# Two levels of HGRN2's token blocks in one product: 2 with 4, and 8 with 16

## The chip, the cores and the metric

The kernel runs on one core of one Trainium2 chip. The metric is the device time of one execution in microseconds; the median of three runs is taken.

## The reference, cut to what matters

One decoder layer: an RMSNorm, a product with `w_in`, two token mixers side by side (RWKV-7 with 16 heads of 64, HGRN2 with 8 heads of 128), a product with `w_out`, the residual and a last norm. There are 1024 tokens of 2048 numbers. The change touches HGRN2 alone:

```python
f = lb + (1.0 - lb) * sigmoid(f_raw)
k = 1.0 - f
Gc = cumsum(log(f))                      # inside chunks of 64 tokens
def step(S, inp):                        # one chunk
    qt, kt, vt, Gt = inp
    inter = einsum('bhtk,bhkv->bhtv', qt * exp(Gt), S)
    E = where(s <= t, exp(Gt[t] - Gt[s]), 0)
    A = einsum('bhtk,bhsk,bhtsk->bhts', qt, kt, E)
    intra = einsum('bhts,bhsv->bhtv', A, vt)
    kdec = kt * exp(G_last - Gt)
    S = S * exp(G_last) + einsum('bhsk,bhsv->bhkv', kdec, vt)
    return S, inter + intra
o = rmsnorm per head (inter + intra) * norm_g * silu(gate)
```

The decay between tokens s and t differs for each of the 128 key dimensions, so A is not one plain product of queries and keys.

## The kernel before, in words

Tokens go through in two halves of 512. The big products (`gemm`, L715) take a column block of 128 of `w_in` at a time, 16 steps each. A step is three matmuls of 128x512 (L732 to L734), since weights and activations are each split into a high and a low part (`whi`, `wlo`, `xs`); the split of the weights is done on ScalarE (L695, high) and VectorE (L705, low). After each step `step` (L788) calls every lane once: lanes are Python generators, one for the scan of RWKV, one for that of HGRN2, one for the group norm and so on. A lane writes down some instructions and then yields; `yield from range(H02)` lets H02 steps pass. So the order on each engine is set when the program is written out: by the lanes' yields and by the numbers in the table at L1041 to L1100. Each engine then runs its own row of instructions in that order and waits for the others by semaphores.

`hgrn_scan` (L246) does one head and one half, so it is called 16 times, eight per half. It works on 8 chunks of 64 tokens, four pairs (`c`) with two chunks (`x`) each. The score matrix A of each chunk is built by blocks. `k` and `qp` hold keys and queries with the decay inside their block of h tokens; `tot` holds the whole decay of each block. For each level the keys of the even blocks get the decay of the odd block behind them (L291, VectorE), the queries of the odd blocks that of the even one ahead (L294, GpSimd), the decays are multiplied in pairs (L298, VectorE), and the block is twice as large. At each level the queries of the odd blocks are multiplied with the keys (L306), and a masked copy (L315, `copy_predicated`, VectorE) takes the valid part from PSUM into AT. There are seven products in a scan: the first (L268) with 96 columns does the diagonal and the pairs of neighbours at once, five with 64 columns the levels 2, 4, 8, 16 and 32, and one (L306 again, four matmuls in place of eight) joins the two chunks of a pair. The 64 columns of each of the eight matmuls hold the odd blocks of both chunks of the pair, though only one of them belongs to the keys; masks leave out the rest.

AT is [128, 4, 128]; the two chunks of a pair lie on its diagonal, and the first product fills them with two masked copies each (L273, L277). Later L347 multiplies AT with the values, and L348 adds queries times state.

Beside it runs the RWKV scan (`rwkv_scan`, L429), eight chunks of 64 tokens one after the other (loop at L598). The prediction names its matmuls by letters: Q is L602 (and L603 beside it), which needs X; T is L611, which needs R, a copy of Q's result on ScalarE (L605); B is L617 (and L622), which needs X written from T by VectorE (L612) and ScalarE (L613); and the X of the next chunk is written from B by VectorE (L619), which also needs SW from GpSimd (L608). Between them stand steps of the big product: one from Q to T, two from T to B, one from B to the next Q. The products of HGRN2 fall between these. After the last chunk comes `rwkv_norm` (L631), and then the next head's LH (L458), which the four products of L467 need.

Of the kernel before, what the change touches and what calls it, by code (L numbers as in the profile page):

```python
# [39 lines left out]
CID, CPK, CBO, CRS, CIQ, NCST = 0, 128, 384, 512, 1024, 1280  # L40
LEVELS = (1, 2, 4, 8, 16, 32)


def shape_constants():
# [7 lines left out]
    c[:, CPK : CPK + 256] = np.concatenate([le, lt, lt, le], axis=1)  # L52
# [5 lines left out]
    m = np.zeros((P, P + 64 * len(LEVELS)), np.float32)  # L58
    m[:, :P] = np.eye(P)
    u = np.arange(64)  # L60
    for l, b in enumerate(LEVELS):
        lo = 2 * b * (u // b)
        m[:, P + 64 * l : P + 64 * (l + 1)] = (p[:, None] >= lo) & (p[:, None] < lo + b)
# [3 lines left out]
class Layer:  # L67
# [8 lines left out]
    def constants(self, cst, msk, vecs, ng):  # L76
# [3 lines left out]
        self.msk = cp.tile([P, P + 64 * len(LEVELS)], U8, name="msk")  # L80
# [42 lines left out]
    def scan_state(self, ctx):  # L123
# [4 lines left out]
        mf = sp.tile([P, P + 64 * len(LEVELS)], F32, name="mf", tag="BK")  # L128
# [7 lines left out]
        self.AT = sp.tile([P, 4, P], F32, name="AT")  # L136
        self.Ep = sp.tile([P, 8, 65], F32, name="Ep")
# [6 lines left out]
        for t in (self.AT, self.TT, self.LH, PX):  # L144
            nc.gpsimd.memset(t, 0.0)
# [100 lines left out]
    def hgrn_scan(self, i, half, f, k, q, v, g, y):  # L246
# [16 lines left out]
        AT = self.AT  # L263
        pl = self.pm()
        plv = pl[:, 0:384].rearrange("p (c n) -> p c n", c=nch)
        for c in range(nch):
            for x in (0, 1):
                nc.tensor.matmul(  # L268
                    plv[hp[x], c, :], lhsT=k[:, c * P + 64 * x : c * P + 64 * x + 64], rhs=q[:, c, x, :],
                    start=True, stop=True,  # L270
                )
        for x in (0, 1):
# [4 lines left out]
            nc.vector.copy_predicated(  # L277
                AT[hp[x], :, 64 * x + 1 : 64 * x + 64 : 2],
                self.msk[hp[x], P + 32 * x : P + 32 * x + 32].unsqueeze(1).broadcast_to([64, nch, 32]),
                plv[hp[x], :, 64:96],  # L280
            )
        yield from range(H01)
        tot = f
        for l in range(1, 8):
            b = 1 << l
            h = b // 2
            n = HT // b
# [13 lines left out]
            if b == P:  # L301
                break
# [743 lines left out]
H04 = 3  # L1046
H05 = 1
H06 = 3
H07 = 3
F00 = 1  # L1050
F01 = 1
F02 = 2
# [217 lines left out]
```

## Time and profile before

| | |
|---|---|
| median of 3 runs | 2367.86 us (2367.67 to 2368.54) |
| profiled execution, its time | 2369.59 us |
| profiled execution, its span | 2367.8 us |
| TensorE busy | 2323.3 us, 98% |
| VectorE busy | 1471.2 us, 62% |
| ScalarE busy | 951.3 us, 40% |
| GpSimd busy | 450.5 us, 19% |
| mean granted TensorE clock | 0.994 of full speed |

A busy TensorE is not a TensorE at its peak, since matmuls overlap and their ends are modelled; starts are the safer reading. The time of a wait is given with the engine that ended it.

### The profile page before, as it was taken

The page shows a single profiled execution, that of the slowest core. Times are in us where ns is not written, and L with a number is a line of the kernel's source. Part 1 is how long each engine was busy: PE and PEld are TensorE (multiplying, and loading weights), DVE is VectorE, ACT ScalarE, POOL GpSimd, SP SyncE. Part 2 cuts the span into 40 slices and gives each one's busy share as a digit, 9 for nine tenths or more (in the row PEclk, how much of TensorE's full clock was granted, in tenths as well). Part 3 has the DMA queues.
Part 4 walks back from the last instruction along what each step waited for, and adds up shares of the span by engine and source line. Part 5 has one row for each costly group of instructions (what it writes and reads, how often), then busy time and mean ns, then how long its engine had stood idle before and what let it go on. Part 6 is the DMA issues. An engine that isn't in the chain of part 4 may idle for free.

```text
span 2367.8 us, 35706 instructions
## 1 busy us (share of the span) xinstructions
PE 2323.3 (98%) x13067; PEld 1912.4 (81%) x13067; DVE 1471.2 (62%) x3104; ACT 951.3 (40%) x2188; POOL 450.5 (19%) x825
## 2 busy tenths in 40 slices
PE   8999999999999999999999999999999998999998
PEld 6888888888888888778888888888888887888888
DVE  5566666666666666656666766676766666435433
ACT  5334444434343434443434343434343434334323
POOL 3022222222121212220212121212121213101000
PEclk9999999999999999999999999999999999999999
DMA  6334334343434252624242424242424243434622
GB/s 185 85 92 92 104 86 109 83 117 82 110 99 128 78 140 62 167 67 105 69 105 68 105 69 104 70 104 70 98 75 96 78 118 116 178 117 142 249 98 98
DMA packets 379663, 249.59 MB, mean 105 GB/s; under 512 B 54368, under 2 KB 346336, under 8 KB 378336
## 3 DMA queue, kind: packets, MB, share of 16 engines
q1 hardware_dynamic: 378912, 243.12, 38.1%
q0 software_dynamic: 576, 4.19, 0.4%
q8 instruction: 103, 1.69, 0.3%
q14 instruction: 72, 0.59, 0.1%
HBM read 221.32 MB, written 25.95 MB: 104 GB/s over the span
## 4 chain that ended last, share of the span: by engine, by line
PE 85%; DVE 7%; ACT 4%; issue 2%; POOL 1%; DMA 1%; SPq 0%; DVEq 0%; POOLq 0%; ACTq 0%
PE g L732 18%; PE g L734 18%; PE g L733 17%; PE m L467 2%; PE m L306 2%; PE c L747 2%; PE c L746 2%; PE c L745 2%; DVE LH L458 2%; PE c L602 2%; PE m L747 1%; PE m L746 1%; PE m L745 1%; PE m L175 1%; PE c L611 1%
## 5 line engine op out<-in xcount | busy, mean ns | idle before, releaser
L732 PE MATMUL g<-xs,whi 128*128 128x512 f32 (+1 forms) x2160 | 904.1, 419 | 0.0
L734 PE MATMUL g<-xs,wlo 128*128 128x512 f32 (+1 forms) x2160 | 848.3, 393 | 1.2 <-DVE wlo L705 1.2
L733 PE MATMUL g<-xs,whi 128*128 128x512 f32 (+1 forms) x2160 | 844.9, 391 | 0.0
L705 DVE TENSOR_TENSOR wlo<-raw,whi 128x512 fp32r<-128x512 f32 (+1 forms) x646 | 469.8, 731 | 271.8 <-ACT whi L695 269.0
L695 ACT CAST whi<-raw 128x512 fp32r<-128x512 f32 (+1 forms) x648 | 393.2, 617 | 387.4 <-PE g L733 218.4
L734 PEld LDWEIGHTS g<-xs,wlo 128*128 128x128 f32 (+1 forms) x2160 | 404.3, 187 | 93.9 <-DVE wlo L705 2.9
L732 PEld LDWEIGHTS g<-xs,whi 128*128 128x128 f32 (+1 forms) x2160 | 406.0, 188 | 76.0 <-issue 0.3
L733 PEld LDWEIGHTS g<-xs,whi 128*128 128x128 f32 (+1 forms) x2160 | 406.6, 188 | 68.3
L608 POOL TENSOR_SCALAR SW<-Xs,Ep 64x64 f32<-64x64 f32 x256 | 135.6, 530 | 302.0 <-DVE Xs L619 290.5
L612 DVE TENSOR_SCALAR Xs<-c,D 64x64 f32<-64x64 f32 x128 | 35.3, 276 | 164.4 <-PE c L611 161.2
L549 DVE TENSOR_TENSOR Xw<-L,X 128x32 f32<-128x32 f32 (+15 forms) x256 | 114.5, 447 | 10.2 <-POOL L L544 5.3
L553 DVE TENSOR_REDUCE X<-Xw 128x16 f32<-128x32 f32 (+15 forms) x256 | 111.7, 436 | 8.8
L624 ACT COPY Y<-c 64x64 f32<-64x64 f32 x256 | 53.0, 207 | 154.6 <-PE c L622 152.4
L294 POOL TENSOR_TENSOR hqp<-hqp,tot 128x256 f32<-128x256 f32 x96 | 64.0, 666 | 193.7 <-PE m L306 163.8
L506 ACT COPY Xs<-m 64x256 f32<-64x256 f32 x64 | 23.6, 368 | 155.8 <-PE m L503 135.1
L619 DVE SCALAR_TENSOR_TENSOR Xs<-c,Ep,SW 64x64 f32<-64x64 f32 x240 | 67.3, 280 | 20.9 <-PE c L617 15.3
L537 POOL MEMSET L<- 128x16 f32 x32 | 3.1, 139 | 397.9 <-DMA L<-lsc 247.9
L567 POOL COPY PX<-Xr 32x256 f32<-32x256 f32 x32 | 12.7, 398 | 340.9 <-DVE Xr L565 340.3
L467 PE MATMUL m<-LH,BK 128*128 128x256 f32 x256 | 66.7, 383 | 7.5 <-DVE LH L458 7.5
L613 ACT ACTIVATE Xs<-c,D 64x64 f32<-64x64 f32 x128 | 39.6, 309 | 81.8 <-DVE Xs L612 79.7
L602 PEld LDWEIGHTS c<-Xs,LH 128*128 128x128 f32 x256 | 39.4, 188 | 39.1 <-DVE Xs L619 37.5
L705 POOL TENSOR_TENSOR xs<-xn,xs 128x512 fp32r<-128x512 f32 x24 | 34.0, 1421 | 190.7 <-ACT xs L944 188.6
(505 smaller groups left out, 3478.4 us busy)
## 6 DMA issues: line engine op xcount, KB each, us to landing
raw<-in_w_in SPq DMA_DIRECT2D x256, 512.0 KB
raw<-in_w_out SPq DMA_DIRECT2D x64, 512.0 KB
L<-lsc SPq DMA_DIRECT2D x16, 512.0 KB
xr<-in_x SPq DMA_DIRECT2D x32, 256.0 KB
xn<-y SPq DMA_DIRECT2D x32, 256.0 KB
out<-h SPq DMA_DIRECT2D x16, 512.0 KB
xr<-in_x SPq DMA_DIRECT2D x8, 512.0 KB
y<-yt SPq DMA_DIRECT2D x16, 256.0 KB
```

The source lines that it names most:

```text
L467: nc.tensor.matmul(pp[:, (c % 2) * 256 : (c % 2 + 1) * 256], lhsT=BK[:, c, :], rhs=LH[:, c].rearrange("p x n -> p (x n)"), start=True, sto ...
L549: nc.vector.tensor_tensor(w[:, :, :, 0:n], Lp[:, k, :, 2 * k :].unsqueeze(1).broadcast_to([P, 8, 2, n]), Xi[:, :, 2 * k :].unsqueeze(2).br ...
L553: nc.vector.tensor_reduce(Xi[:, :, 2 * k : 2 * k + 2].unsqueeze(3), w[:, :, :, 0:n], axis=AX.X, op=ALU.add)
L602: nc.tensor.matmul(ps[:, 0:P], lhsT=LH[:, c, 0, :], rhs=X[:, c, :], start=True, stop=True)
L608: nc.gpsimd.tensor_scalar_mul(SW[hp[h], :], X[hp[h], c, hp[h]], wc[hp[h]])
L695: nc.scalar.copy(hi[:, :, 0:n], raw)
L705: low()
L732: nc.tensor.matmul(ps[e], lhsT=hi[:, k, 0:n], rhs=x[:, 0, :], start=kk == 0, stop=False)
L733: nc.tensor.matmul(ps[e], lhsT=hi[:, k, 0:n], rhs=x[:, 1, :], start=False, stop=False)
L734: nc.tensor.matmul(ps[e], lhsT=lo[:, k, 0:n], rhs=x[:, 0, :], start=False, stop=kk == NK - 1)
L745: mm(ps, lhsT=x[:, 0, ts], rhs=hi, start=first, stop=False)
L746: mm(ps, lhsT=x[:, 0, ts], rhs=lo, start=False, stop=False)
```

## The change

The seven levels are no longer done one by one. The levels 2 and 4 share one product, and so do 8 and 16. For each pair, queries of three kinds are put side by side in `q`, 32 columns each for each chunk of 64 tokens: the odd blocks of the smaller level (kind 0), and, of the odd blocks of the larger level, the queries for the key block right ahead (kind 1) and for the one ahead of that (kind 2). Kinds 0 and 1 are copies on ScalarE, kind 2 is a multiply on GpSimd that adds the decay of the block between. The products are now taken for each chunk with its own queries alone, so level 32 has 32 columns. The masked copies write into a new tile AD, [128, 4, 64], in which the two chunks of a pair stand one below the other; two copies on ScalarE bring it into AT at the end. The constants tile and the masks become smaller, and the group norm uses two rows in place of three.

```diff
-LEVELS = (1, 2, 4, 8, 16, 32)
+LEVELS = ((2, 4), (8, 16), (32,))
...
-        for x in (0, 1):
+        def products(n, rhs):
+            pl = self.pm()
+            for c in range(nch):
+                for x in (0, 1):
+                    o = c * P + 64 * x
+                    nc.tensor.matmul(
+                        pl[hp[x], c * n : (c + 1) * n], lhsT=k[:, o : o + 64], rhs=rhs(c, x), start=True, stop=True
+                    )
+            return pl[:, 0 : nch * n].rearrange("p (c n) -> p c n", c=nch)
+
+        def take(pl, n, b, mask):
             nc.vector.copy_predicated(
-                AT[hp[x], :, hp[x]], self.msk[hp[x], hp[x]].unsqueeze(1).broadcast_to([64, nch, 64]),
-                plv[hp[x], :, 0:64],
+                AD.rearrange("p c (n e j) -> p c n e j", e=2, j=b)[:, :, :, 1, :],
+                self.msk[:, mask : mask + 32].rearrange("p (n j) -> p n j", j=b).unsqueeze(1).broadcast_to([P, nch, 32 // b, b]),
+                pl[:, :, n : n + 32].rearrange("p c (n j) -> p c n j", j=b),
             )
...
+        pl = products(96, lambda c, x: q[:, c, x, :])
+        nc.vector.copy_predicated(AD, self.msk[:, 0:64].unsqueeze(1).broadcast_to([P, nch, 64]), pl[:, :, 0:64])
+        take(pl, 64, 1, MONE)
         yield from range(H01)
...
+        for level in LEVELS:
+            b = level[0]
+            keys(b // 2)
+            queries(b // 2)
+            tot = totals(b)
+            yield from range(H02)
+            if len(level) == 1:
+                pl = products(32, lambda c, x: qp[:, c * P + 64 * x + 32 : c * P + 64 * x + 64])
+                yield from range(H03)
+                take(pl, 0, b, mask)
+                mask += 32
+                continue
+            nc.scalar.copy(kind(0, b), odd(b))
+            queries(b)
+            yield from range(H08)
+            nc.scalar.copy(kind(1, 2 * b), odd(2 * b))
+            n = 16 // b
+            nc.gpsimd.tensor_tensor(
+                kind(2, 2 * b), odd(2 * b),
+                tot.rearrange("p (g m e) -> p g m e", g=8, e=4)[:, :, :, 1:2].broadcast_to([P, 8, n, 2 * b]), op=ALU.mult,
             )
+            yield from range(H09)
+            pl = products(96, lambda c, x: q[:, c, x, :])
+            yield from range(H03)
+            take(pl, 0, b, mask)
+            take(pl, 32, 2 * b, mask + 32)
+            take(pl, 64, 2 * b, mask + 64)
+            mask += 96
+            keys(b)
+            tot = totals(2 * b)
+            yield from range(H03)
+        keys(32)
+        queries(32)
+        tot = totals(64)
+        yield from range(H02)
...
+        nc.scalar.copy(AT[0:64, :, 64:P], pl[0:64, 0:256].rearrange("p (c j) -> p c j", c=nch))
+        keys(64)
+        queries(64)
+        tot = totals(P)
+        for x in (0, 1):
+            nc.scalar.copy(AT[hp[x], :, hp[x]], AD[hp[x]])
+        yield from range(H02)
...
+H08 = 2
+H09 = 2
```

`keys`, `queries` and `totals` are the multiplies of L291, L294 and L298 under a name. The yields of a scan become a few more, so what stands behind them comes a little later among the steps of the big product.

On TensorE the prediction speaks of the fourth chunk of the RWKV scan. Before, from T to B:

```order
L611 MATMUL c<-R,TT 128x128
L306 MATMUL m<-hqp,hk 64x64 x8
L732 MATMUL g<-xs,whi 128x512
L733 MATMUL g<-xs,whi 128x512
L734 MATMUL g<-xs,wlo 128x512
L732 MATMUL g<-xs,whi 128x512
L733 MATMUL g<-xs,whi 128x512
L734 MATMUL g<-xs,wlo 128x512
L617 MATMUL c<-Xs,BKt 128x128
L622 MATMUL c<-Xs,PR 128x128
```

Now, from B to the next Q (L666 is B, L651 is Q):

```order
L666 MATMUL c<-Xs,BKt 128x128
L671 MATMUL c<-Xs,PR 128x128
L284 MATMUL m<-hqp,hk 64x32 x8
L781 MATMUL g<-xs,whi 128x512
L782 MATMUL g<-xs,whi 128x512
L783 MATMUL g<-xs,wlo 128x512
L651 MATMUL c<-Xs,LH 128x128
```

The product of level 32 has moved from between T and B to between B and the next Q; between T and B only two steps of the big product are left there.

On VectorE, the rows of the same chunk before, from its L612 to the update of X (L189 is the projection of k):

```order
L612 TENSOR_SCALAR Xs<-c,D_825 64x64
L315 COPY_PREDICATED AT<-msk,m 128x8x32
L705 TENSOR_TENSOR wlo<-raw,whi 128x512
L291 TENSOR_TENSOR hk<-hk,tot_1692 128x8x32
L298 TENSOR_TENSOR tot_1748<-tot_1692 128x8
L189 SCALAR_TENSOR_TENSOR k__1724<-g,omu,shift 128x512
L619 SCALAR_TENSOR_TENSOR Xs<-c,Ep,SW 64x64 x2
```

And now, from the update of X in the third chunk (L668 is L619, L661 is L612, L754 is wlo):

```order
L668 SCALAR_TENSOR_TENSOR Xs<-c,Ep,SW 64x64 x2
L291 COPY_PREDICATED AD<-msk,m 128x16x8
L291 COPY_PREDICATED AD<-msk,m 128x8x16 x2
L307 TENSOR_TENSOR hk<-hk,tot_1598 128x32x8
L315 TENSOR_TENSOR tot_1687<-tot_1598 128x32
L307 TENSOR_TENSOR hk<-hk,tot_1687 128x16x16
L315 TENSOR_TENSOR tot_1703<-tot_1687 128x16
L661 TENSOR_SCALAR Xs<-c,D_827 64x64
L754 TENSOR_TENSOR wlo<-raw,whi 128x512
L202 SCALAR_TENSOR_TENSOR k__1714<-g,omu,shift 128x512
L668 SCALAR_TENSOR_TENSOR Xs<-c,Ep,SW 64x64 x2
```

Three masked copies, two key multiplies and two totals now stand in one run ahead of L661, and none of them between L661 and the next L668.

On ScalarE, from the end of the chunks' preparation to the first chunk's R, before (L605 is R, L187 the shift, L202 the gate):

```order
L590 COPY TT<-m 32x8x32 x2
L695 CAST whi<-raw 128x512
L187 ACTIVATE shift<-g,vec 128x512
L202 ACTIVATE th<-g__1524 128x512
L605 COPY R<-c 128x128
```

And now, up to the second chunk's R (L335 and L338 collect kinds 0 and 1):

```order
L639 COPY TT<-m 32x8x32 x2
L744 CAST whi<-raw 128x512
L335 COPY hq<-hqp 128x8x32
L200 ACTIVATE shift<-g,vec 128x512
L338 COPY hq<-hqp 128x8x32
L215 ACTIVATE th<-g__1524 128x512
L654 COPY R<-c 128x128
L744 CAST whi<-raw 128x512
L662 ACTIVATE Xs<-c,D_827 64x64
L673 COPY Y<-c 64x64 x2
L654 COPY R<-c 128x128
```

Two collecting copies stand ahead of the first chunk's R; the second chunk's R has none ahead of it.

On GpSimd, at the end of the scan before (L336 clears the first state, L184 is the first column of the shift for r, L356 and L357 HGRN2's norm, L638 the first of the group norm):

```order
L356 TENSOR_SCALAR hss<-hss 128x4
L357 TENSOR_TENSOR hss<-hss,mhalf 128x4
L184 MEMSET shift 128x1
L193 COPY carry<-shift 128x1
L638 TENSOR_SCALAR gn<-gn 128x8
```

And now:

```order
L197 MEMSET shift 128x1
L206 COPY carry<-shift 128x1
L405 TENSOR_SCALAR hss<-hss 128x4
L406 TENSOR_TENSOR hss<-hss,mhalf 128x4
L687 TENSOR_SCALAR gn<-gn 128x8
```

The shift's memset has moved ahead of HGRN2's norm.

## Rows read from the trace of the kernel before

**Rows 1.** The page: busy time, share of the span and instructions of TensorE.

```profile
PE 2323.3 (98%) x13067; PEld 1912.4 (81%) x13067; DVE 1471.2 (62%) x3104; ACT 951.3 (40%) x2188; POOL 450.5 (19%) x825
```

**Rows 2.** TensorE's timeline: start, length (us), line; the idle time before it in brackets.

```profile
156.84 0.42 PE L602 MATMUL c<-Xs,LH 128*128 128x128 f32 x2
...
158.01 0.38 PE L611 MATMUL c<-R,TT 128*128 128x128 f32 x2
...
171.36 0.49 PE L602 MATMUL c<-Xs,LH 128*128 128x128 f32 x2 [0.16 <-DVE Xs L619]
...
209.72 1.10 PE L467 MATMUL m<-LH,BK 128*128 128x256 f32 x4 [0.71 <-DVE LH L458]
```

**Rows 3.** The list of waits, whole span: us in total, times, longest.

```profile
PE m L467 <- DVE LH L458: 7.5, 14, 0.7
...
PE c L602 <- DVE Xs L619: 6.3, 15, 1.9
```

**Rows 4.** TensorE's timeline around one group of eight 64-column products.

```profile
148.63 0.40 PE L734 MATMUL g<-xs,wlo 128*128 128x512 f32 x1
148.96 0.69 PE L306 MATMUL m<-hqp,hk 128*64 128x64 f32 x16
149.57 0.50 PE L732 MATMUL g<-xs,whi 128*128 128x512 f32 x1
149.91 0.40 PE L733 MATMUL g<-xs,whi 128*128 128x512 f32 x1
150.14 0.40 PE L734 MATMUL g<-xs,wlo 128*128 128x512 f32 x1
```

**Rows 5.** TensorE's timeline: 32-column products of RWKV, then the 96-column group.

```profile
142.91 1.11 PE L578 MATMUL m<-Xc,PX 64*64 64x32 f32 x16
143.96 0.88 PE L268 MATMUL m<-hq,hk 128*64 128x96 f32 x16
144.77 0.50 PE L732 MATMUL g<-xs,whi 128*128 128x512 f32 x1
```

**Rows 6.** TensorE's timeline: the scan's last group, four products.

```profile
172.92 0.68 PE L306 MATMUL m<-hqp,hk 128*64 128x64 f32 x8
```

**Rows 7.** Groups by line and shape, whole span: busy us, mean ns, idle before.

```profile
L315 DVE COPY_PREDICATED AT<-msk,m 128x256 f32<-128x256 uint8 x80 | 40.2, 502 | 39.6 <-PE m L306 39.6
...
L277 DVE COPY_PREDICATED AT<-msk,m 64x128 f32<-64x128 uint8 x32 | 14.1, 440 | 1.1
...
L298 DVE TENSOR_TENSOR tot<-tot 128x128 f32<-128x128 f32 x16 | 4.7, 296 | 0.0
...
L261 ACT COPY hq<-hqp 128x256 f32<-128x256 f32 x16 | 6.9, 428 | 2.7 <-DVE hqp L260 2.7
...
L294 POOL TENSOR_TENSOR hqp<-hqp,tot 128x256 f32<-128x256 f32 x96 | 64.0, 666 | 193.7 <-PE m L306 163.8 <-issue 29.9
```

**Rows 8.** VectorE's timeline, the second chunk of the first scan.

```profile
158.50 0.28 DVE L612 TENSOR_SCALAR Xs<-c,D 64x64 f32<-64x64 f32 x1 [1.79 <-PE c L611]
159.05 0.44 DVE L315 COPY_PREDICATED AT<-msk,m 128x256 f32<-128x256 uint8 x1 [0.28 <-PE m L306]
159.39 0.97 DVE L705 TENSOR_TENSOR wlo<-raw,whi 128x512 fp32r<-128x512 f32 x1
160.29 0.41 DVE L291 TENSOR_TENSOR hk<-hk,tot 128x256 f32<-128x256 f32 x1
160.62 0.18 DVE L298 TENSOR_TENSOR tot<-tot 128x32 f32<-128x32 f32 x1
160.84 0.60 DVE L619 SCALAR_TENSOR_TENSOR Xs<-c,Ep,SW 64x64 f32<-64x64 f32 x2
```

**Rows 9.** ScalarE's timeline, R of the same chunk.

```profile
157.34 0.27 ACT L605 COPY R<-c 128x128 f32<-128x128 f32 x1 [0.58 <-PE c L602]
```

**Rows 10.** VectorE's timeline at the end of the first scan.

```profile
194.45 0.75 DVE L189 SCALAR_TENSOR_TENSOR r__1955<-g,omu,shift 128x512 f32<-128x512 f32 x1 [2.83 <-POOL shift L184]
```

**Rows 11.** GpSimd's timeline at the same place.

```profile
193.32 1.05 POOL L357 TENSOR_TENSOR hss<-hss,mhalf 128x4 f32<-128x4 f32 x1
```

More of the change, by code (lines that the diff above doesn't have):

```diff
@@ L38 @@
 )
-CID, CPK, CBO, CRS, CIQ, NCST = 0, 128, 384, 512, 1024, 1280
-LEVELS = (1, 2, 4, 8, 16, 32)
+CID, CPK, CBO, CRS, CIQ, NCST = 0, 128, 256, 384, 896, 1152
+LEVELS = ((2, 4), (8, 16), (32,))
+MONE, MLEV, NMSK = 64, 96, 320
 def shape_constants():
@@ L57, in shape_constants @@
     c[:, CIQ : CIQ + 256] = iq.reshape(P, 256)
[L58 to L63, printed above, removed]
+    m = np.zeros((P, NMSK), np.float32)
+    k = (p % 64)[:, None]
+    m[:, 0:64] = k == np.arange(64)
+    u = np.arange(32)
+    between = lambda lo, n: (k >= lo) & (k < lo + n)
+    m[:, MONE : MONE + 32] = between(2 * u, 1)
+    o = MLEV
+    for b in LEVELS:
+        m[:, o : o + 32] = between(2 * b[0] * (u // b[0]), b[0])
+        o += 32
+        if len(b) == 2:
+            lo = 2 * b[1] * (u // b[1])
+            m[:, o : o + 32] = between(lo + b[0], b[0])
+            m[:, o + 32 : o + 64] = between(lo, b[0])
+            o += 64
     return c, m
@@ L136, in scan_state @@
         self.AT = sp.tile([P, 4, P], F32, name="AT")
+        self.AD = sp.tile([P, 4, 64], F32, name="AD")
         self.Ep = sp.tile([P, 8, 65], F32, name="Ep")
@@ L143, in scan_state @@
         self.Pb, self.Xh = PX[0:64], PX[64:P]
-        for t in (self.AT, self.TT, self.LH, PX):
+        for t in (self.AT, self.AD, self.TT, self.LH, PX):
             nc.gpsimd.memset(t, 0.0)
@@ L262, in hgrn_scan @@
         yield from range(H00)
[L263 to L266, printed above, removed]
-            for x in (0, 1):
[L268 to L272, printed above, removed]
+        AT, AD = self.AT, self.AD
+        def products(n, rhs):
[7 more added lines that the diff above has]
+            return pl[:, 0 : nch * n].rearrange("p (c n) -> p c n", c=nch)
@@ new lines, in hgrn_scan, with keys, queries @@
+        pairs = lambda x: x.rearrange("p (n e) -> p n e", e=2)
+        blocks = lambda x, j: x.rearrange("p (n e j) -> p n e j", e=2, j=j)
+        def keys(h):
+            kv, n = blocks(k, h)[:, :, 0, :], HT // (2 * h)
+            nc.vector.tensor_tensor(kv, kv, pairs(tot)[:, :, 1:2].broadcast_to([P, n, h]), op=ALU.mult)
+        def queries(h):
+            qv, n = blocks(qp, h)[:, :, 1, :], HT // (2 * h)
+            nc.gpsimd.tensor_tensor(qv, qv, pairs(tot)[:, :, 0:1].broadcast_to([P, n, h]), op=ALU.mult)
@@ new lines, in hgrn_scan @@
+        keys(32)
+        queries(32)
+        tot = totals(64)
+        yield from range(H02)
+        pl = self.pm()
+        for c in range(nch):
+            nc.tensor.matmul(
+                pl[0:64, c * 64 : (c + 1) * 64], lhsT=k[:, c * P : c * P + 64], rhs=qp[:, c * P + 64 : (c + 1) * P],
+                start=True, stop=True,
+            )
+        yield from range(H03)
+        nc.scalar.copy(AT[0:64, :, 64:P], pl[0:64, 0:256].rearrange("p (c j) -> p c j", c=nch))
+        keys(64)
```

62 lines of the change are left out of this document (14 added, 48 removed).

## The prediction, made before the changed kernel had run

> **What bounds the kernel now.** I read the page first. TensorE is busy for 98% of the span, the next engine, VectorE, for 62% [rows 1]. That share flatters TensorE, because a matmul of the big products is drawn 0.39 us long while the next one starts 0.23 us later [rows 4]. So I went on to the timeline of TensorE alone, and read start times, not lengths. Nearly everywhere one matmul starts as soon as the one before lets it. Where TensorE waits, the waits are few and come back with each head: at the start of a chunk of the RWKV scan for the state X from VectorE, and at L467 for LH from VectorE [rows 2]. The list of waits puts them at 6.3 us in 15 times and 7.5 us in 14 times [rows 3]; each is 0.16 us longer in truth, because the matmul before it is drawn that much too long (0.39 less 0.23). TensorE's instruction stream is the bound, and work taken out of it comes off the span unless a wait takes its place. The gain is therefore worked out in two parts: TensorE work removed, and waits that go or come.
>
> **The products of the HGRN2 scan.** A product group of eight 64-column matmuls costs more than its own time, because the switch to half-width products breaks the rhythm of the big ones. From the L734 before it to the second big matmul behind it 1.28 us pass [rows 4]; without the group these would be two steps of 0.23, 0.46 us. So a group costs 0.82 us. The 96-column group L268 occupies 0.81 us from its first start to the next big matmul [rows 5], the 64-column one 0.61 [rows 4]: 0.20 more, so 1.02 us. The last group has four products, all on one half of the array, and is drawn 0.68 us long [rows 6], the group of eight on both halves 0.69 [rows 4]: also 0.82. The changed kernel's eight 32-column products are not in this trace. Taking 0.20 per 32 columns off again gives 0.62; no saving gives 0.82. L578 has 32 columns and needs 1.05 us for its 16 passes [rows 5], not less than the 64-column group, so I take 0.82 and keep the other 3.2 us (16 x 0.20) for the range.
> Before, one scan has one group of 96 columns and six at 0.82: 1.02 + 4.92 = 5.94 us. After, three of 96 columns, one of 32 and the last: 3.06 + 0.82 + 0.82 = 4.70. That is 1.24 us less, and with 16 scans **19.8 us** of TensorE work, all of it in line with the big products.
>
> **What the other engines get.** ScalarE gains per scan four copies that collect queries, like L261 at 0.43 us, and two copies from AD to AT of half the partitions, which I price at the same 0.43. GpSimd gains two multiplies like L294 at 0.67 [rows 7]. VectorE keeps nine masked copies, seven of them now of 128 elements a partition. Such a copy lies between 0.30 (a 128-element multiply, L298) and 0.44 us (the 128-element masked copy L277) [rows 7]; the present 256-element one takes 0.50 on average. None of these engines is full, so only places count where TensorE waits for them.
> The Trainium skill, "VectorE: DVE Perf Modes", section on the TRN2 errata, gives 120 cycles plus one per element at 0.96 GHz for a copy out of PSUM, so 0.26 us as an estimate for 128 elements; the 0.44 us of L277 contradicts it here. By the page the three copies in a row would be 0.5 us shorter than by that row and could delay nobody, which would make the sum 0.6 us larger; the sum below uses neither value, but steps between the rows.
>
> *Three masked copies in a row.* They follow each of the two combined products, on VectorE, where the RWKV chain's updates of X queue behind them. Steps from start to start there: masked copy 0.34, wlo 0.90, key multiply 0.33, total 0.22 [rows 8]; a short masked copy then takes 0.20 (0.34 less the 0.14 between 0.44 and 0.30) to 0.34. First place, the chunk with the first group: T (L611) at 0; VectorE is free at 0.77 (L612 starts 0.49 behind T and takes 0.28) [rows 2, 8]; wlo to 1.67, masks to 2.27 or 2.69, key and total to 2.82 or 3.24. The product B (L617) now stands at 0.22 + 1.02 + 6 x 0.23 = 2.62, and X can be updated 0.49 later, at 3.11. So VectorE is in time or 0.13 late. Its two updates take 0.60, to 3.71 or 3.84, and Q (L602) is due at 2.62 + 0.45 + 0.69 = 3.76. A wait of 0 to 0.08, so 0 to 1.3 us in all; I take 0.6. Second place: masks, two keys and two totals stand between the update of X in the third chunk and L612 of the fourth, 1.7 to 2.1 us, where VectorE now idles for 1.79 [rows 8]. L612 may be 0.3 late, but it ends 0.77 behind T where nothing is late, and B comes 0.22 + 6 x 0.23 = 1.60 behind T even in a chunk without a group. Nothing.
>
> *ScalarE in front of R.* R (L605) must be copied between Q and T. It ends at 157.34 + 0.27 = 157.61 and T starts at 158.01 [rows 2, 9]: 0.40 to spare. In the first chunk two of the collecting copies stand ahead of R, with the shift of the gate between them, and the second waits for GpSimd. TensorE also comes there 0.82 earlier, as one group ahead of it is gone. Bounds: nothing, or both copies, 0.86 us. In favour of the low end, VectorE's gate projection, behind which R waits, loses a masked copy, a key multiply and a total ahead of it, 0.34 + 0.33 + 0.22 = 0.89. I take 0.2 a scan, **3.2 us** lost; the range keeps 13.8. The other two collecting copies come behind L613 and behind R, where nobody waits for ScalarE. Products wait for GpSimd's last multiply, but it has two steps of the big product, 1.4 us, for 0.67.
>
> *Waits that go.* Twelve of the 15 waits for X are like that at 171.36 [rows 2]: VectorE has the masked copy, wlo, key, total and the projection of k ahead of X. In the new order wlo and the projection alone stand there, and a 32-column group (0.82) stands on TensorE ahead of Q. 12 x (0.16 + 0.16) = **3.8 us** go. The wait at L467 is the end of a long chain: VectorE's projection of r waits 2.83 us for a memset on GpSimd [rows 10], which stands behind the power of hss, 1.05 us [rows 11], which waits for HGRN2's outputs. All of the group norm and then LH come behind. In the new order this memset stands ahead of hss, so the norm starts up to 2.8 us earlier; HGRN2's end is later by two or three steps and gives about 1 us back. The wait is 0.71 + 0.16 = 0.87, so I let it go: 7.5 + 14 x 0.16 = **9.7 us**.
>
> **The sum.** 19.8 + 3.8 + 9.7 - 0.6 - 3.2 = 29.5 us. The profiled execution took 2369.6, the median of the runs is 2367.9; the difference is a sum against one execution of the same program, so I carry it over to the median: 2367.9 - 29.5 = 2338.4, **2338 us**.
>
> **Rivals.**
> *Only the work goes.* The waits for X and LH are ends of latency chains, and a faster TensorE reaches them sooner, or other late ends stand just behind. Then 19.8 - 0.6 - 3.2 = 16.0 remain: 2352 us. Against it speaks that the new order takes known causes away, not only slack.
> *VectorE's bunches become the bound.* The three masks take 0.44 each without overlap, 0.3 us more in each of two places, 9.6 us, and the old waits stay: 16.0 - 9.6 = 6.4 us, 2361. L277's 0.44 speaks for it, the 1.79 us of idle time against. The Trainium skill, "TensorEngine Tiling (Array Packing)", section Performance Considerations, warns of this: tiling speeds up the products and not the copies out of PSUM. The trace shows masked copies within the engine's idle time so far.
> *The chain becomes the bound, no change.* The second and fourth chunks lose their group, and if the chain Q, R, T, X, B, X took as long as TensorE did with it, 1.24 us a scan would come back as waits: about 2368. Against it: R is ready 0.77 behind Q [rows 2, 9], VectorE's half of X 0.77 behind T and its update 1.09 behind B [rows 8], 2.6 us in all, while a chunk without a group still has four steps of three big matmuls on TensorE, 12 x 0.23 = 2.8 us, and its own five small pairs beside them.
> *Slower: ScalarE is stopped by GpSimd.* A collecting copy stands ahead of R and waits in ScalarE's queue for a multiply of 0.67 us, with R, the whi casts and the Y copies behind it. One such place costs 0.43 + 0.67 - 0.40 = 0.70 us. From two of the four places a scan (1.4 against 1.24) the kernel is slower; at all four it loses 16 x 2.8 = 44.8 and ends at 2367.9 - 19.8 + 44.8 = 2393. The order shows both copies of the second pair away from R, which speaks against it.
>
> **How the numbers follow.** Forecast 0.64, only work 0.22, bunches 0.06, no change 0.04, slower 0.04. The forecast's own low end: 29.5 + 3.2 (32 columns) + 3.8 (no new wait) + about 5 for smaller waits of the same kind that I did not list, 41.5: 2326. The upper end of the range must take in the second case and the higher price of R in it, so 2358. What lies above (bunches, no change, slower) and a little of the other two make the 2 in 10. A measurement of this kernel can tell about 0.2% from no change, 4.7 us: faster 0.92, same 0.04, slower 0.04.
>
> **What would show it.** On TensorE's timeline three groups of 0.81 us a scan in place of one, and two of 0.61 in place of six; if the 32-column one is shorter, the price was too high. In the list of waits LH at L467 near zero, X below 5 us, R up by at most a few us. A product waiting for GpSimd or ScalarE, T waiting for R by more than 0.5 us in each scan, or VectorE's updates of X starting more than 0.3 us behind B would show the terms wrong. If LH still waits 7 us, the chain behind HGRN2's end was read wrongly, and the second case holds.

## The result, and the profile after

The changed kernel takes **2330.4 us** (median of five runs, 2329.9 to 2330.6) against 2368.5 us for the kernel before on the same chip; the ratio is 0.9837 with a 95% interval of 0.9824 to 0.9851. The prediction was 2338 us, so it named about three quarters of the gain: 29.5 us of 38. The profiled span fell from 2367.8 to 2328.8 us.

The page's line of busy times answers to [rows 1]. TensorE has 512 matmuls less and is as "busy" as before; VectorE's busy time fell by 18 us, ScalarE's and GpSimd's rose:

```profile
PE 2293.4 (98%) x12555; PEld 1897.1 (81%) x12555; DVE 1452.8 (62%) x3104; ACT 981.4 (42%) x2284; POOL 471.0 (20%) x858
```

The list of waits of TensorE answers to [rows 3] (us in total, times, longest). LH is not in it any more, and X (L651, which was L602) has 3 waits in place of 15. New in the list is T (L660) at its head, put down partly to SW from GpSimd and partly to R from ScalarE:

```profile
PE c L660 <- POOL SW L657: 3.5, 7, 0.5
PE c L660 <- ACT R L654: 2.5, 6, 0.5
PE c L651 <- DVE Xs L668: 1.5, 3, 0.6
```

The product groups on TensorE's timeline (start, length, line), the answer to [rows 4] and [rows 5]. The combined 96-column group goes from 152.73 to the next big matmul at 153.54, 0.81 us; the 32-column group from 168.67 to 169.25, 0.58, hardly less than the 0.61 of 64 columns:

```profile
152.34 0.46 PE L660 MATMUL c<-R,TT 128*128 128x128 f32 x2 [0.41 <-ACT R L654]
152.73 0.88 PE L284 MATMUL m<-hq,hk 128*64 128x96 f32 x16
153.54 0.50 PE L781 MATMUL g<-xs,whi 128*128 128x512 f32 x1
...
168.67 0.66 PE L284 MATMUL m<-hqp,hk 128*64 128x32 f32 x16
169.25 0.50 PE L781 MATMUL g<-xs,whi 128*128 128x512 f32 x1
...
206.67 1.03 PE L516 MATMUL m<-LH,BK 128*128 128x256 f32 x4
```

The last of these rows is the four products that waited 0.71 us for LH in [rows 2]: no idle time stands before it now. The groups of instructions by line and shape show the new masked copy, and ScalarE's collecting copies, at the prices the prediction bounded with [rows 7] (0.30 to 0.44, and 0.43):

```profile
L291 DVE COPY_PREDICATED AD<-msk,m 128x128 f32<-128x128 uint8 x128 | 42.7, 334 | 3.9 <-PE m L284 0.2
...
L335 ACT COPY hq<-hqp 128x256 f32<-128x256 f32 x32 | 13.2, 412 | 0.4
L338 ACT COPY hq<-hqp 128x256 f32<-128x256 f32 x32 | 13.1, 408 | 6.5 <-POOL hqp L311 3.2 <-POOL shift L197 3.2
```

**Where the 39 us went.** The list of waits counts only what exceeds the drawn ends, so I also went over all of TensorE's starts. For every stretch of other matmuls between two big ones I took the time from the start of the big matmul ahead to the start of the second one behind, less two steps of 0.2265 us. The fastest stretch of a kind (over several kernels) is its work, and what another of the kind takes more, if over 0.04 us, is a wait, put down to the place at which the stretch begins. In us over the whole run:

| | before | after | difference |
|---|---|---|---|
| work of the other matmuls | 469.3 | 451.5 | -17.8 |
| waits at Q, most of them for X | 21.9 | 6.7 | -15.2 |
| wait for LH | 10.8 | 0 | -10.8 |
| wait of the group norm's first product for Y | 1.7 | 0 | -1.7 |
| waits at T | 5.2 | 9.2 | +4.0 |
| waits at B | 0 | 3.2 | +3.2 |
| all other waits | 19.5 | 20.0 | +0.5 |
| all of it, with what is under 0.04 us | 531.5 | 492.6 | -38.9 |

The total agrees with the spans (-39.0). So a little under half is work, and the rest is waits: 28 us gone, 7 us new. The experiments ask where these waits come from, and what the work consists of.

### The profile page after: what moved, and what is told of

Its sections match the earlier page's. It is cut to its first block, busy times and chain, and to the rows that moved or that the text cites. A ratio compares the mean times of both kernels' runs of the same rounds, so it can differ in the third digit from the quotient of the medians.

```text
span 2328.8 us, 34832 instructions
## 1 busy us (share of the span) xinstructions
PE 2293.4 (98%) x12555; PEld 1897.1 (81%) x12555; DVE 1452.8 (62%) x3104; ACT 981.4 (42%) x2284; POOL 471.0 (20%) x858
## 4 chain that ended last, share of the span: by engine, by line
PE 89%; DVE 4%; DMA 3%; issue 2%; ACT 1%; POOL 1%; SPq 0%; POOLq 0%; DVEq 0%; ACTq 0%
PE g L781 19%; PE g L783 19%; PE g L782 19%; PE m L516 2%; PE m L284 2%; PE c L796 2%; PE c L794 2%; PE c L795 2%; PE m L796 1%; PE m L794 1%; PE m L795 1%; PE c L660 1%; PE c L651 1%; PE g L794 1%; PE g L796 1%
## 5 line engine op out<-in xcount | busy, mean ns | idle before, releaser
L754 DVE TENSOR_TENSOR wlo<-raw,whi 128x512 fp32r<-128x512 f32 (+1 forms) x646 | 449.1, 698 | 296.9 <-ACT whi L744 295.6
L602 DVE TENSOR_REDUCE X<-Xw 128x16 f32<-128x32 f32 (+15 forms) x256 | 111.8, 437 | 8.8
L661 DVE TENSOR_SCALAR Xs<-c,D 64x64 f32<-64x64 f32 x128 | 35.2, 275 | 123.7 <-PE c L660 93.6
L668 DVE SCALAR_TENSOR_TENSOR Xs<-c,Ep,SW 64x64 f32<-64x64 f32 x240 | 67.5, 281 | 57.2 <-PE c L666 51.9
L754 POOL TENSOR_TENSOR xs<-xn,xs 128x512 fp32r<-128x512 f32 x24 | 34.1, 1423 | 188.7 <-ACT xs L993 186.5
L654 ACT COPY R<-c 128x128 f32<-128x128 f32 x128 | 33.8, 264 | 80.4 <-PE c L651 80.4
```

The source lines that it names most:

```text
L602: nc.vector.tensor_reduce(Xi[:, :, 2 * k : 2 * k + 2].unsqueeze(3), w[:, :, :, 0:n], axis=AX.X, op=ALU.add)
L754: low()
```

## Experiments

**1. The LH chain in the kernel before.** The prediction said that a memset of one column on GpSimd, behind the power of hss [rows 11], holds VectorE [rows 10] and with it LH. Here only that column moves to VectorE:

```diff
-        if half == 0:
-            nc.gpsimd.memset(s[:rows, 0:1], 0.0)
-        else:
-            nc.gpsimd.tensor_copy(s[:rows, 0:1], self.carry[:rows, col : col + 1])
         nc.scalar.activation(s[:rows, 1:], ps[:rows, :], AF.Copy, scale=mu[:rows])
         yield
+        if half == 0:
+            nc.vector.memset(s[:rows, 0:1], 0.0)
+        else:
+            nc.vector.tensor_copy(s[:rows, 0:1], self.carry[:rows, col : col + 1])
         nc.vector.scalar_tensor_tensor(
```

> The kernel before, in which one instruction of the token shift changes its engine and place: the first column (a memset in the first half, a copy of the carry in the second) is written by VectorE right ahead of the multiply-add that reads it, and no longer by GpSimd. The products of HGRN2 stay as they were. Theory: the wait of L467 for LH (9.7 us with the modelled overlap) is the end of a chain that hangs on this memset alone, which stands in GpSimd's queue behind the power of hss; so it goes without any change of the products, and some of the small waits at T and at the gate with it: 9 to 12 us less than before, about 2358. Rival: the group norm's own start at HGRN2's outputs sets LH; then the wait stays near 9 us and the time near 2368.

Measured: 2366.0 us, ratio 0.9987 (0.9978 to 0.9997). The wait for LH is gone from the list of waits, as the theory says, but the time is only 3.4 us shorter, not 10. Its list has what came in exchange:

```profile
PE c L602 <- DVE Xs L619: 10.7, 16, 1.9
...
PE c L611 <- ACT R L605: 5.1, 13, 0.7
```

By the accounting above LH fell from 10.8 to 1.6 us and the norm's wait from 1.7 to 0, while T rose from 5.2 to 8.7 and X by 5.8. VectorE's timeline in the first chunk shows why: masked copy, wlo, key and total run without a gap up to the column, so the gate's projection, behind which R waits, is later by it:

```profile
151.50 0.28 DVE L298 TENSOR_TENSOR tot<-tot 128x128 f32<-128x128 f32 x1
151.72 0.06 DVE L186 MEMSET shift<- 128x1 f32 x1
151.91 0.75 DVE L189 SCALAR_TENSOR_TENSOR g__1524<-g,omu,shift 128x512 f32<-128x512 f32 x1
```

From the total to the projection 0.41 us pass, where the kernel before needs 0.21 (151.35 to 151.56). The cause of the LH wait is shown; that it can be removed at no price is not.

**2. The same edit in the changed kernel.** In the changed kernel T waits, and the timelines of the engines in the first chunk offer two causes. The first: on GpSimd the column of the gate's shift (L197) stands behind the query multiply, which waited for ScalarE's collecting copy.

```profile
149.61 0.94 POOL L311 TENSOR_TENSOR hqp<-hqp,tot 128x256 f32<-128x256 f32 x1 [6.42 <-ACT hq L335]
150.49 0.10 POOL L197 MEMSET shift<- 128x1 f32 x1
...
150.62 0.75 DVE L202 SCALAR_TENSOR_TENSOR g__1524<-g,omu,shift 128x512 f32<-128x512 f32 x1 [0.68 <-POOL shift L197]
...
150.58 0.41 ACT L338 COPY hq<-hqp 128x256 f32<-128x256 f32 x1 [0.46 <-POOL shift L197]
151.41 0.63 ACT L215 ACTIVATE th<-g__1524 128x512 f32<-128x512 f32 x1 [0.42 <-DVE g__1524 L202]
151.94 0.25 ACT L654 COPY R<-c 128x128 f32<-128x128 f32 x1
```

VectorE idles 0.68 us for the column, the tanh L215 waits for VectorE, and R stands behind it. The second cause, the prediction's, is the collecting copy L338 ahead of the tanh and R. The edit is that of experiment 1.

> The changed kernel with the same edit: the first column of the token shift is written by VectorE, not by GpSimd. Theory: the wait of T for R (8.1 us over the run) comes from GpSimd's queue, where the shift's memset stands behind the multiply of the queries, which waits for a collecting copy on ScalarE; VectorE's half of the shift, the gate's tanh and then R come behind. With the edge off that queue T waits at most 0.1 us a time, and the time is 6 to 8 us shorter than that of the changed kernel, about 2323. Rival, the mechanism of the prediction: ScalarE's own time for the collecting copies in front of R makes T late; then T still waits 0.4 us or more in most heads, and the time stays within 2 us of 2330.

Measured: **2322.2 us**, ratio to the kernel before 0.9802 (0.9787 to 0.9816), 8.2 us below the changed kernel. T falls from 9.2 to 2.6 us by the accounting; the list has no wait of T left. The same place now:

```profile
149.71 0.75 DVE L202 SCALAR_TENSOR_TENSOR g__1524<-g,omu,shift 128x512 f32<-128x512 f32 x1 [0.21 <-ACT shift L196]
...
150.13 0.41 ACT L338 COPY hq<-hqp 128x256 f32<-128x256 f32 x1 [0.46 <-POOL hqp L311]
150.50 0.63 ACT L215 ACTIVATE th<-g__1524 128x512 f32<-128x512 f32 x1
```

The tanh now starts as L338 lets it, so the prediction's cause is second in line and worth what is left, at most 2.6 us. What cost 0.2 us a time in experiment 1 costs nothing here, as the masked copy, key and total no longer stand ahead of the column on VectorE. This is the fastest kernel of the study.

**3. The collecting copy away from R.** The opposite test: the copy of kind 1 a step later, the column still on GpSimd.

```diff
-            nc.scalar.copy(kind(1, 2 * b), odd(2 * b))
             n = 16 // b
             nc.gpsimd.tensor_tensor(
...
-            yield from range(H09)
+            yield
+            nc.scalar.copy(kind(1, 2 * b), odd(2 * b))
+            yield from range(H09 - 1)
```

> The changed kernel with the second collecting copy of each combined product (kind 1, ScalarE) one step of the big product later, so that it no longer stands ahead of the gate's tanh and of R in ScalarE's queue; the memset of the shift stays on GpSimd behind the queries. Theory: T waits for R because of that memset; the copy alone is hidden in the same time, T goes on waiting 0.5 us or more in each of 13 heads, 7 to 8 us in all, and the time stays within 1.5 us of 2330. Rival, the step of the prediction: the copies ahead of R make the wait; then it goes, and the time is 2323 to 2325.

Measured: 2342.8 us, ratio 0.9888 (0.9873 to 0.9902), slower than the changed kernel by 12.4 us. The copy now stands behind R, and T waits 9.2 us as before, so the copy was not its cause. The loss was expected by neither theory: at the second combined product the copy now stands behind X on ScalarE (L663), which needs T, and the product comes one step of the big product behind T.

```profile
PE m L284 <- ACT hq L344: 10.6, 16, 0.7
...
162.14 0.31 ACT L663 ACTIVATE Xs<-c,D 64x64 f32<-64x64 f32 x1 [0.50 <-DVE Xs L662]
162.47 0.40 ACT L344 COPY hq<-hqp 128x256 f32<-128x256 f32 x1
...
163.02 0.88 PE L284 MATMUL m<-hq,hk 128*64 128x96 f32 x16 [0.66 <-ACT hq L344]
```

**4. One group for each level again.** All levels singly, seven groups a scan as before, but with the narrower products and AD of the change.

```diff
-LEVELS = ((2, 4), (8, 16), (32,))
+LEVELS = ((2,), (4,), (8,), (16,), (32,))
...
-                pl = products(32, lambda c, x: qp[:, c * P + 64 * x + 32 : c * P + 64 * x + 64])
+                own = lambda c, x: blocks(qp[:, c * P + 64 * x : c * P + 64 * x + 64], b)[:, :, 1, :]
+                pl = products(32, own)
+                take(pl, 0, b, mask)
                 yield from range(H03)
-                take(pl, 0, b, mask)
...
+        nc.scalar.copy(AT[0:64, :, 64:P], pl[0:64, 0:256].rearrange("p (c j) -> p c j", c=nch))
         yield from range(H03)
-        nc.scalar.copy(AT[0:64, :, 64:P], pl[0:64, 0:256].rearrange("p (c j) -> p c j", c=nch))
```

The last lines put the masked copy, and the copy of the last group, right behind their products again, as they stand in the kernel before.

> The changed kernel with every level done singly again: seven products a scan as before, but each level with its own chunk's 32 columns in place of 64, and diagonal blocks kept in AD. Theory: a group costs nearly the same whatever its width (64 columns 0.615 us, 32 columns 0.588 from first start to the next big matmul), so narrower products alone bring 5 x 0.03 x 16 = 2 us, the order of the scan is that of before, and the waits for X and LH stay: about 2362 to 2367. Rival: what gained was the narrower columns or the masks of 128 elements, not the number of groups: then half of the 38 us or more comes here too, 2349 or less.

Measured: 2365.9 us, ratio 0.9985 (0.9975 to 0.9995), and the work of the other matmuls is 2.1 us less than before. The waits for LH and X are there as before (the norm's as well):

```profile
PE m L517 <- DVE LH L508: 7.7, 14, 0.8
...
PE c L652 <- DVE Xs L669: 4.2, 16, 0.8
```

So half the columns and masks of half the size bring 2 to 3 us together. The gain hangs on the number of groups and on the order.

**5. Each combined product twice.** What does a group cost without the change to half-width products and back?

```diff
-        def products(n, rhs):
+        def products(n, rhs, times=1):
...
-            for c in range(nch):
+            for c in times * list(range(nch)):
...
-            pl = products(96, lambda c, x: q[:, c, x, :])
+            pl = products(96, lambda c, x: q[:, c, x, :], 2)
```

> The changed kernel with each of the two combined products of 96 columns issued twice in a row into the same place, so that its eight pairs stand on TensorE twice; nothing else is changed. It prices columns without a second switch of layout, and shows whether TensorE's stream is the bound at these places. Theory: it is; eight matmuls in four simultaneous pairs on the two halves of the array, 0.0825 us from pair to pair, 0.33 us more for each product, and 2 x 16 of them: 10.6 us more than the changed kernel, about 2341; were the eight not side by side on the halves, 0.66 us each and 21 us, 2351. Rival: the chain through R, T and X is the bound there and has room; then it is less than 3 us, 2330 to 2333.

Measured: 2350.7 us, ratio 0.9923 (0.9908 to 0.9938), 20.3 us above the changed kernel. TensorE is the bound there, and the second of the two prices holds. The reason that the expectation gave for it is wrong: the trace lists 16 half-width matmuls for eight products, two passes each, and pairs of them on the two halves do start together, 0.0825 us apart. I had counted one pass. The doubled group on TensorE's timeline:

```profile
152.95 1.54 PE L284 MATMUL m<-hq,hk 128*64 128x96 f32 x32
154.42 0.50 PE L781 MATMUL g<-xs,whi 128*128 128x512 f32 x1
```

1.47 us to the next big matmul, against 0.81 for one: 0.66 us are the eight products themselves and 0.15 the way back to the big ones. Of the 0.2 us that a group costs beside this, half lies ahead of it (in [rows 4] 0.33 us from L734 to the group, where two big ones are 0.23 apart) and half behind the first big matmul (0.34 from L732 to L733). At 64 and at 32 columns the steps between pairs are 0.058 us both; only the first step of a group differs (0.11 and 0.08). Below 64 columns a step doesn't get shorter, which is why experiment 4 gains so little, while a step of 96 columns (0.08) replaces two of 64 (0.12).

**6. The tail of the scan, both ways.** The change also moves the end of the HGRN2 scan two or three steps later. The number H04 sets this alone: 1 in place of 3 in the changed kernel, 5 in place of 3 in the kernel before.

```diff
-H04 = 3
+H04 = 1
```

> The changed kernel with one number altered: the tail of the HGRN2 scan (from the two last multiplies to the group norm) starts two steps of the big product earlier, as far as the number H04 sets it (1 in place of 3). TensorE's work is the same. On GpSimd it puts the power of hss back ahead of the memset that opens the shift of r. Theory: that order alone made the wait of L516 for LH; it comes back with 0.5 to 0.9 us in each of 14 heads, 7 to 12 us, and the time is 2337 to 2342. Rival: the wait went because fewer product groups end the scan's chain earlier or later; then it stays away and the time is within 2 us of 2330.

> The kernel before with the tail of its HGRN2 scan two steps later (H04 5 in place of 3), products untouched. On GpSimd the memset of the shift of r stands ahead of the power of hss, as in the changed kernel. Theory: the wait of L467 for LH (9.7 us) goes and nothing else is late, since VectorE gets no instruction more: about 2359. Rival: the later tail pushes the outputs of HGRN2 and the group norm, the wait only changes its releaser, or comes back at T and Q as it did when VectorE wrote the first column: 2365 or more.

Measured: the changed kernel with the early tail 2351.9 us (0.9927, 0.9912 to 0.9942), 21.5 us slower; the kernel before with the late tail 2353.1 us (0.9931, 0.9914 to 0.9948), 16.2 us faster than its own runs. The wait for LH comes back in the first (the row below) and is not in the list of the second. GpSimd's rows of the changed kernel with the early tail have the order of the kernel before, the memset behind the power of hss:

```profile
PE m L516 <- DVE LH L507: 7.5, 14, 0.7
...
191.91 1.05 POOL L406 TENSOR_TENSOR hss<-hss,mhalf 128x4 f32<-128x4 f32 x1
192.91 0.10 POOL L197 MEMSET shift<- 128x1 f32 x1
```

Both are larger than expected, by 10 and 6 us, and in both the rest stands at Q and at the norm: Q goes from 6.7 to 15.7 us and the norm's wait from 0 to 1.8 in the first, Q from 21.9 to 18.4 and the norm from 1.7 to 0 in the second. The norm stands behind the projection of [rows 10], as LH does. What Q waits for stands in other rows, at two places. In the last chunk VectorE's update of X (L619, L668 after) stands behind two of HGRN2's state updates (L340) in the kernel before, and Q comes 0.22 us late; in the changed kernel one of them is gone from there and the update waits for B instead (VectorE and TensorE before, VectorE after):

```profile
187.28 0.33 DVE L340 SCALAR_TENSOR_TENSOR hst<-hst,tot,m 128x128 f32<-128x128 f32 x1
187.54 0.57 DVE L619 SCALAR_TENSOR_TENSOR Xs<-c,Ep,SW 64x64 f32<-64x64 f32 x2
...
188.17 0.49 PE L602 MATMUL c<-Xs,LH 128*128 128x128 f32 x2
...
185.68 0.58 DVE L668 SCALAR_TENSOR_TENSOR Xs<-c,Ep,SW 64x64 f32<-64x64 f32 x2 [0.48 <-PE c L666]
```

In the seventh chunk ScalarE's copy of HGRN2's keys (L328) stands ahead of that of RWKV's Y in the kernel before, and L603 waits for Y, 0.3 us in each of 15 scans:

```profile
180.84 0.59 ACT L328 COPY hkt<-m 128x512 f32<-128x512 f32 x1
...
182.81 0.42 ACT L624 COPY Y<-c 64x64 f32<-64x64 f32 x2
```

The changed kernel has the copy behind Y; with the early tail its state product (L381) then waits 0.3 us for the copy, with H04 = 3 next to nothing waits there. So the early tail costs the changed kernel 10.8 us at LH, 1.8 at the norm, 4.6 at Q of the last chunk and 4.1 in the seventh, 21.3 of the 21.5 us. The late tail in the kernel before takes the first three of these away; the seventh chunk's wait stays, with the copy still ahead of Y. No run moves the copy alone.

**7. Both edits, and a still later tail.** The column on VectorE (experiment 2) with H04 = 1, and with H04 = 5.

> The kernel with both edits at once: the changed kernel, the first column of the shift written by VectorE, and the tail of the HGRN2 scan two steps earlier (H04 1 in place of 3). The earlier tail alone cost the changed kernel 21.5 us; of these its trace has 10.8 as the wait of L516 for LH, the rest as waits for X at the last chunk and in the neighbours of HGRN2's output products. Theory: the wait for LH is the memset on GpSimd behind the power of hss and cannot come back when VectorE writes that column; the other part comes back: about 10 us more than with the column on VectorE alone (2322.2), 2330 to 2335. Rival: the earlier tail costs by where it stands, whatever engine writes the column: 2340 or more.

> The changed kernel with the first column of the shift on VectorE and the tail of the HGRN2 scan two steps later still (H04 5 in place of 3). It asks whether the later tail has more to give. Theory: no; the wait for LH is gone already, and what is left of waits (B 3.5 us, T 2.6, X 6.2) stands far from the tail: within 2 us of 2322, or a few us more where HGRN2's outputs now reach the next head too late. Rival: each step later takes several us of switches between products out: 2315 or less.

Measured: 2332.5 us (0.9845, 0.9828 to 0.9861) and 2331.1 us (0.9840, 0.9825 to 0.9855). With the early tail LH costs 1.8 us in place of 10.8, and the norm doesn't wait, so nearly all of these two was the memset's place; the other part comes back at Q of the seventh and the last chunk, as the theory said (6.2 to 13.5 us). So those two waits don't hang on the memset: in experiment 1 too, without it, Q of the last chunk waits 5.0 us, against 4.9 in the kernel before. With the later tail nothing is gained, and LH waits again, 6.5 us by the accounting, though no memset is in the way:

```profile
PE m L516 <- DVE LH L507: 2.5, 6, 0.5
...
193.74 0.43 POOL L405 TENSOR_SCALAR hss<-hss 128x4 f32<-128x4 f32 x1 [4.22 <-ACT th L404]
```

GpSimd gets HGRN2's outputs 1.9 us later than in experiment 2 (191.88 there); that the norm can't make this up is the likely reason, not a tested one. Of the three places tried, that of the change is the best.

**8. The masked copies twice.** How much room is left on VectorE behind the combined products?

```diff
-            take(pl, 0, b, mask)
-            take(pl, 32, 2 * b, mask + 32)
-            take(pl, 64, 2 * b, mask + 64)
+            for _ in (0, 1):
+                take(pl, 0, b, mask)
+                take(pl, 32, 2 * b, mask + 32)
+                take(pl, 64, 2 * b, mask + 64)
```

> The changed kernel with the three masked copies behind each of the two combined products issued twice (six copies in a row in place of three, the same result); TensorE's work is the same. It measures how much room VectorE has at the two places where the prediction counted with 0 to 0.13 us. Three copies are 0.87 us more, from start to start. Theory: there is room neither at the first place (X is written 0.45 behind B, 12 ns before it is needed) nor at the second (the X of the fourth chunk is already late by 0.13): each scan loses some 0.7 and 0.85 us, 16 x 1.55 = 25 us in all, 2355. Rival, by the 1.79 us of idle time that the prediction saw at the second place: only the first place loses, 11 us, 2341; or neither, 2330.

Measured: 2359.3 us, ratio 0.9958 (0.9943 to 0.9973), 28.9 us above the changed kernel, a little more than the 25 of the theory. Both places pay in each of 16 scans: by the accounting X at Q rises by 15.3 us and X at B by 15.6.

```profile
PE c L667 <- ACT Xs L663: 14.6, 16, 1.0
PE c L652 <- DVE Xs L669: 12.9, 19, 1.1
```

On VectorE's timeline the three copies more take 1.14 us at the first place and 1.01 at the second, and they cost 0.92 and 0.98: VectorE has 0.2 us of room at the first place and none at the second, with 62% busy on average.

## Why the prediction came out as it did

**Work: 19.8 said, 17.8 measured.** The mechanism and the prices hold: 1.02 us for a 96-column group among big matmuls, 0.98 behind T, 0.81 for one of 64. Two prices were off. The last group costs 0.69 us in the kernel before, where it stands between T and the projection of wahh, and 0.80 after, where it stands behind B; I had 0.82 for both. The 32-column group costs 0.78 behind B, not 0.82. With these the count of groups gives 18.6; the other 0.8 I can't place. The first group is 0.81 in both kernels, not 1.02, and drops out.

**LH: 9.7 said, 10.8 measured**, for the reason given: experiments 1, 6 and 7 remove and restore it by the memset's place. The size comes out too: behind a wait the second start of L467 is 0.08 us late as well (209.72 to 210.01, where 0.22 is usual), so 7.5 + 14 x (0.16 + 0.08) = 10.9. What I missed is that the same wait on VectorE also feeds the norm's first product.

**X: 3.8 said, 15.2 measured; this is the term that failed.** I counted twelve waits of one kind from the list and wrote "about 5 for smaller waits of the same kind that I did not list" into the low end only. Taken apart by chunk (to within 0.6 us of the table), the waits at Q fall from 6.4 to 2.3 us in the fifth chunk, where my twelve stand, from 4.5 to 2.4 in the second, from 4.7 to 0.1 in the seventh and from 4.9 to 0.3 in the last. The twelve are still there with the late tail alone (experiment 6), so the new order of the products takes them away, as predicted; that their 3.8 us come out is luck. Each costs 0.44 us, since the second start behind it is 0.1 late too, and 0.13 of it stays, so 0.31 goes; I had 0.32 with nothing left. Three long waits (at 775, 1011 and 1994 us) shrink by 2.8 together. What I hadn't seen is the seventh and the last chunk, 9.2 us: 0.3 to 0.4 us a time, nearly all drawn as less than 0.15 us of idle time, so that the list of waits doesn't name them. They are neither of the same kind nor small: experiment 6 puts them on HGRN2's key copy and state updates, which stand ahead of Y and X. The tail as a whole (LH, the norm, Q of the last chunk, in the changed kernel the seventh too) is worth 16 to 21 us, the merged products with their new waits some 17 (experiment 6, with the early tail: 2351.9 against 2368.5). I had made the products the main thing and the tail a by-product; they are equal.

**R and T: 3.2 lost said, 4.0 measured, by another cause.** I put the loss on collecting copies in front of R. Experiments 2 and 3 show the cause to be GpSimd: the query multiply waits there for the copy that frees its input, and the gate's column stands behind it. I had left that queue out, though the change adds a wait ahead of the multiply. T waits 0.7 us in 14 of the 16 scans by the accounting, 0.4 in the kernel before: the sign that I had named for a wrong term, and it came. The relief that I counted on, 0.89 us less on VectorE ahead of the projection, is real, but VectorE spent 0.68 of it waiting.

**VectorE's bunches: 0.6 said, 3.2 measured.** At the first place X is in time, as said: B at 155.03, the update at 155.45, Q at 156.17 without idle time. At the second place I wrote "Nothing", and B waits in 14 of the 16 scans, 0.23 us by the accounting. The total behind the copies takes 0.60 us where 0.16 would be expected from the kernel before, so VectorE's half of X comes late; ScalarE's half, which I had left out, waits for that one and ends 0.67 us after that one starts, and B waits for ScalarE. In the scan at 1491 us, where GpSimd's multiply starts behind the total and not ahead of it, the total takes 0.17 us and B doesn't wait (timelines of VectorE, GpSimd, ScalarE and TensorE, then VectorE and GpSimd in that scan):

```profile
166.77 0.60 DVE L315 TENSOR_TENSOR tot<-tot 128x16 f32<-128x16 f32 x1
167.30 0.27 DVE L661 TENSOR_SCALAR Xs<-c,D 64x64 f32<-64x64 f32 x1
...
166.57 0.77 POOL L311 TENSOR_TENSOR hqp<-hqp,tot 128x256 f32<-128x256 f32 x1 [0.52 <-ACT whi L744]
...
167.66 0.31 ACT L662 ACTIVATE Xs<-c,D 64x64 f32<-64x64 f32 x1 [1.14 <-DVE Xs L661]
...
168.02 0.49 PE L666 MATMUL c<-Xs,BKt 128*128 128x128 f32 x2
...
1491.56 0.17 DVE L315 TENSOR_TENSOR tot<-tot 128x16 f32<-128x16 f32 x1
...
1491.64 0.63 POOL L311 TENSOR_TENSOR hqp<-hqp,tot 128x256 f32<-128x256 f32 x1 [0.81 <-ACT whi L744]
```

The masked copies themselves take 0.29 us each from start to start at this place and 0.34 at the first, the high end of the 0.20 to 0.34 that I took. The estimate of 0.26 us by the Trainium skill, "VectorE: DVE Perf Modes", the section on the TRN2 errata, is nearer to them than the 0.44 of L277, by which I had called the page contradicted.

**The rivals.** "Only the work goes" (2352) is ruled out by the waits that went; the changed kernel with its early tail, in which LH, the norm and Q of the last two chunks wait as before, does land near it, at 2351.9. "VectorE's bunches become the bound" (2361) is ruled out by the time and by the 3.2 us that they came to, though experiment 8 shows how little was missing. "The chain becomes the bound" is ruled out in the chunks that it named: T of the second and the fourth, which lost their group, never waits, and only B of the fourth does. Experiment 5 adds that work on TensorE is paid in full in the first and the third. The slower case, ScalarE stopped by GpSimd, exists as a mechanism at one of its four places: L338 waits 0.46 us for GpSimd with the tanh and R behind it (experiment 2), and costs at most the 2.6 us that T has left there.

## What to carry to other kernels

Before a change of order is priced, follow each wait that stands on an engine off the critical path to everything queued behind it: here one memset of a single column on GpSimd held a projection on VectorE, and with it two waits on TensorE, 12.5 us against the 17.8 of saved work. Put such small instructions on the engine that reads the result, where that engine has room ahead of it (8.2 us gained in the changed kernel, 3.4 in the kernel before, where it had none). Look also at what another lane's copies and updates stand ahead of: HGRN2's key copy and state updates, moved by two or three steps, took 9 us of waits out of the RWKV scan. And read waits from the starts of all instructions of the bounding engine: these 9 us were 0.3 to 0.4 us a time, drawn as less than half of that, and the list of waits didn't name them.

## What the runs showed of the hardware

The total over 16 elements a partition takes 0.16 us in all 16 scans of the kernel before, and 0.60 in 15 of 16 after; in the row at 166.77 above it ends at 167.37, with GpSimd's multiply, which began ahead of it and ends at 167.34. In the one scan in which the multiply begins behind it, it takes 0.17. In the same way wlo takes 0.69 us alone and 0.94 (median of 91) while GpSimd multiplies queries in the kernel before. VectorE's X updates, with one operand in PSUM, keep their 0.28 us beside GpSimd. The Trainium skill, "SBUF — State Buffer", section "Who interferes with whom", has it so: a VectorE instruction with two inputs in SBUF contends with a GpSimd instruction that reads SBUF, and whoever comes second is blocked; the trace agrees.

Below 64 columns a half-width product of fp32 gets no cheaper: from one pair of passes to the next 0.083 us at 96 columns, 0.058 at 64 and 0.058 at 32 (medians over the run; the first step of a group is longer). A group of four products on one half of the array alone takes as long as eight on both, 0.61 us to the next matmul, since its eight single passes are 0.058 us apart as well.

A wait of TensorE costs more than it is drawn: the matmul ahead is drawn 0.16 us longer than its step, and the start after the one that waited is late again, by 0.1 us at Q (0.21 in place of 0.11 at 171.36) and by 0.08 at L467.
